# Branch A's first scores between the last q tiles, and denominators fetched by GpSimd and applied three tiles later

## The chip, the cores and the metric

The kernel runs on one core of a Trainium2 chip. The metric is device microseconds of one execution: the median of 3 runs was 1786.32 us (1786.25 to 1786.35). A core has five engines that each run their own queue in order: TensorE (PE; its weight loads, PEld, overlap its matmuls), VectorE (DVE), ScalarE (ACT), GpSimd (POOL) and SyncE (SP). In this kernel SP and POOL issue the transfers between the chip's memories. An instruction that waits holds up all that stands behind it in its queue.

## The reference, cut to what matters

One encoder layer over 1024 tokens of 1024 numbers. The change touches attention branch A:

```
h = RMSNorm(x);  z = h @ W_in                      # columns: A: q,k,v | B: q,k,v | gates
q = rope(rmsnorm(q)) * 128 ** -0.5                 # 8 heads of 128
k = rope(rmsnorm(k))                               # 2 heads of 128, each serves 4 q heads
pr = softmax(q @ k.T);  A = pr @ v                 # over all 1024 tokens
x += (sigmoid(gate_A) * (A @ W_oA) + sigmoid(gate_B) * (B @ W_oB)) @ W_o
```

Before it stand the projections and branch B, after it the output projections, the MLP and a gated embedding.

## The kernel before

All products are made in fp32r, three matmuls for one (`mm3`): each operand is split into a high part (a copy on ACT, line 236) and a low part (a subtraction on DVE, line 237), and all the matmuls of products stand at line 240.

`qkv_a` projects k and v of branch A (block 0) and then q in two blocks of four heads (blocks 1 and 2), each over 8 tiles of 128 tokens. A tile is 24 matmuls into one PSUM bank; ACT then squares it head by head (860) for the norm, and DVE applies the rotary tables (813, 818, 820). Two tiles later its `turn` runs: PE transposes it (834), ACT copies the result out of PSUM (839), SP stores it as `s_qd`. The banks of tiles are `ps_a`, those of turns `ps_t`. The last two turns are left over for the attention.

`attend_a` works through 16 units (8 heads times two halves of 512 queries), and a last pass without new scores. A unit has four score tiles: `scores(u, j)` is 6 matmuls, a maximum over 1024 scores on DVE (925), its product with the norm (927), an exponential on ACT (929) that fills a probability buffer and adds up a column of denominators. In pass u, step j, PE makes score tile j of unit u, then the transposes of two key chunks of unit u-1 (`weights`, 935, 8 matmuls; ACT and DVE split them, 236 and 237, tile `rp`), then the products with v of the two chunks before (`values`, 6 matmuls). The first transposes of unit u-1 need all four of its exponentials. `finish(u)` copies the unit's output out of PSUM (949), takes the reciprocal of its denominators (951), has SP store these as four columns to `s_rd` and load them back as one row on all partitions (`rb`), and then multiplies (956) and splits the result into `oA` (tile `ro`).

PE's order is the program's. The other engines' orders, and those of SP and POOL, are set by a scheduler from its own costs, so the text of the program does not show them. Tiles live in stacked regions on two sides of the on-chip memory; a region that is closed frees its place for the next one, which then waits for the readers of the old. In the kernel before, the score tiles' PSUM (banks 0 to 3) takes in the banks 2 and 3 of the turns.

## Time and profile before

| | |
|---|---|
| median of 3 runs | 1786.32 us |
| profiled execution, its own time | 1784.23 us |
| its span | 1782.5 us |
| PE busy in the span | 1734.3 us, 97% |
| DVE, ACT, POOL busy | 1255.6, 794.7, 391.1 us |
| tiles of q, block 2, until | 576.19 us |
| attention of branch A, unit to unit | 14.45 us |

Times inside the profile count from the span's start. A row of the timeline gives start and length in us, engine, line, operation, the tile written and the tiles read; in brackets stands how long the engine stood idle before it and what ended that. Matmuls are pipelined, so a group's length reaches a little into the next group's start; the chain that ended last cuts the groups without overlap. The clock (PEclk) is 1.00 at 2.4 GHz and 0.50 at 1.2 GHz.

### The profile page before, as it was taken

Reading aid. Unit: us, or ns where it says so; the run is one execution under the profiler, and the core shown is the slowest. Engines: PE = TensorE matmul, PEld = TensorE weight load, DVE = VectorE, ACT = ScalarE, POOL = GpSimd, SP = SyncE. Lnnn points to the kernel's source line nnn. Section 1 sums busy time; section 2 is a strip of 40 time slices with the busy share of each in tenths; the row PEclk is TensorE's granted clock in tenths of the full one; section 3 lists DMA queues with packets and bytes.
Section 4 is the critical chain, followed back from the end, with each engine's and each line's share of the span. In section 5 each row is a group of like instructions: output and inputs, shape, how many; then the busy total and the mean of one; then the engine's idle time right before and its main releaser. Section 6 shows DMA issues by size and latency. Waiting matters only on the chain.

```text
span 1782.5 us, 22922 instructions
## 1 busy us (share of the span) xinstructions
PE 1734.3 (97%) x8451; PEld 1434.9 (80%) x8451; DVE 1255.6 (70%) x2096; ACT 794.7 (45%) x1385; POOL 391.1 (22%) x242
## 2 busy tenths in 40 slices
PE   6999999999999899999999979999999999999997
PEld 5888888877888788888888868888888888888786
DVE  7546655476865888875446588667668999998664
ACT  6333334267333677775332346545547333330232
POOL 0242422010000000000001134322426677722000
PEclk9999999999999999999999989999999999999999
DMA  6243234476154322215433135656667222266111
GB/s 218 71 159 133 102 109 152 134 243 192 36 155 130 72 42 22 33 19 142 139 123 134 72 106 189 208 194 209 223 253 253 102 94 96 74 205 240 64 41 38
DMA packets 147552, 232.77 MB, mean 131 GB/s; under 512 B 27204, under 2 KB 94628, under 8 KB 147440
## 3 DMA queue, kind: packets, MB, share of 16 engines
q1 hardware_dynamic: 141152, 208.86, 36.7%
q0 software_dynamic: 6288, 22.44, 3.7%
q8 instruction: 67, 1.10, 0.3%
q14 instruction: 45, 0.37, 0.1%
HBM read 162.90 MB, written 71.51 MB: 132 GB/s over the span
## 4 chain that ended last, share of the span: by engine, by line
PE 65%; DVE 1%; issue 1%; ACT 0%; DVEq 0%; ACTq 0%
PE psum L240 61%; PE psum L935 3%; DVE rc L237 0%; PE psum L1370 0%; PE psum L1061 0%; ACT fp L929 0%; DVE base L925 0%; DVE hb L237 0%; ACT hb L236 0%; PE psum L1360 0%; DVE fx L1055 0%; DVE fsum L1306 0%; DVE fx L1077 0%; PE psum L834 0%; ACT rc L236 0%
## 5 line engine op out<-in xcount | busy, mean ns | idle before, releaser
L240 PE MATMUL psum<-rh,rh 128*128 128x512 f32 (+1 forms) x1428 | 336.2, 389 | 1.6 <-ACT rh L236 1.1
L240 PEld LDWEIGHTS psum<-rh,rh 128*128 128x128 f32 x1428 | 261.1, 190 | 59.5 <-issue 5.9
L240 PE MATMUL psum<-rc,rc 128*128 128x512 f32 x1320 | 304.2, 390 | 2.0 <-issue 1.6
L240 PEld LDWEIGHTS psum<-rc,rc 128*128 128x128 f32 x1320 | 246.7, 188 | 55.2 <-issue 4.2
L152 POOL TENSOR_TENSOR base<-base 128x512 f32<-128x512 f32 x17 | 25.9, 1525 | 776.8 <-DMA base<-in_w_ff 620.7
L240 PE MATMUL psum<-ht,rh 128*128 128x512 f32 x624 | 145.7, 389 | 0.0
L240 PE MATMUL psum<-hc,rc 128*128 128x512 f32 x576 | 137.9, 389 | 0.0
L240 PEld LDWEIGHTS psum<-ht,rh 128*128 128x128 f32 x624 | 117.1, 188 | 24.3
L236 ACT ACTIVATE rh<-base 128x512 fp32r<-128x512 f32 (+1 forms) x77 | 61.2, 808 | 147.9 <-PE psum L240 116.6
L240 PEld LDWEIGHTS psum<-hc,rc 128*128 128x128 f32 x576 | 108.1, 188 | 22.4
L237 DVE TENSOR_TENSOR rh<-base,rh 128x512 fp32r<-128x512 f32 (+1 forms) x77 | 77.4, 1014 | 62.6 <-PE psum L240 39.0
L240 PE MATMUL psum<-ro,rwt 128*128 128x512 f32 x480 | 109.0, 389 | 0.0
L240 PEld LDWEIGHTS psum<-ro,rwt 128*128 128x128 f32 x480 | 90.1, 188 | 18.7
L210 DVE TENSOR_TENSOR fw<-fw,psum 128x512 f32<-128x512 f32 x91 | 74.3, 817 | 43.6 <-PE psum L240 42.5
L240 PE MATMUL psum<-rp,kv 128*128 128x512 f32 x384 | 103.5, 405 | 0.0
L925 DVE TENSOR_REDUCE base<-psum 128x1 f32<-128x1024 f32 x64 | 78.3, 1224 | 35.6 <-PE psum L240 35.6
L240 PE MATMUL psum<-kv,rq 128*128 128x512 f32 x384 | 99.2, 395 | 2.5 <-ACT fp L929 1.6
L240 PE MATMUL psum<-hb,rc 128*128 128x512 f32 x384 | 94.6, 396 | 5.8 <-DVE hb L237 5.8
L1236 DVE TENSOR_TENSOR facc<-facc,psum 128x1024 f32<-128x1024 f32 x84 | 98.7, 1208 | 0.0
L237 DVE TENSOR_TENSOR rc<-fsum,rc 128x1024 fp32r<-128x1024 f32 x56 | 93.7, 1701 | 4.6 <-ACT rc L236 4.6
L236 ACT ACTIVATE rc<-fsum 128x1024 fp32r<-128x1024 f32 x56 | 57.4, 1055 | 85.3 <-issue 65.9
L240 PE MATMUL psum<-ha,rc 128*128 128x512 f32 x384 | 91.4, 394 | 0.0
(275 smaller groups left out, 3057.4 us busy)
## 6 DMA issues: line engine op xcount, KB each, us to landing
base<-in_w_ff SPq DMA_DIRECT2D x20, 1024.0 KB, 6.2
base<-in_w_in SPq DMA_DIRECT2D x13, 1024.0 KB, 5.1
base<-in_w_in SPq DMA_DIRECT2D x20, 512.0 KB, 4.7
s_u<-rfa SPq DMA_DIRECT2D x18, 512.0 KB, 2.9
fg<-s_gd SPq DMA_DIRECT2D x16, 512.0 KB, 5.9
s_wgs<-base SPq DMA_DIRECT2D x32, 256.0 KB, 2.0
s_gd<-fw SPq DMA_DIRECT2D x14, 512.0 KB, 3.1
rfa<-s_u SPq DMA_DIRECT2D x6, 1024.0 KB, 4.9
```

The costliest lines, as they stand in the source:

```text
L152: g.tensor_tensor(out=s1, in0=a21, in1=a22, op=ALU.add)
L210: self.nc.vector.tensor_tensor(out=self.c[out], in0=self.c[a], in1=self.p[i], op=op)
L236: self.nc.scalar.activation(hi, src, AF.Copy)
L237: (eng or self.nc.vector).tensor_tensor(out=lo, in0=src, in1=hi.bitcast(F32), op=ALU.subtract)
L240: self.nc.tensor.matmul(out, lhsT=lhsT, rhs=rhs, start=start, stop=stop)
L925: nc.vector.tensor_reduce(out=nm, in_=ps, axis=AX.X, op=ALU.max, negate=True)
L935: nc.tensor.transpose(pp[:, j * P:(j + 1) * P], probs[j][:, kc * P:(kc + 1) * P], self.ident)
L1236: v.tensor_tensor(out=o, in0=o, in1=ps, op=ALU.add)
```

## The change

Five things are edited. (1) `attend_a` becomes a generator that `qkv_a` advances in block 2 after the tiles 3 to 7: at tile 3 it takes its regions, and the four score tiles of unit 0 are made after the tiles 4, 5, 6 and 7. The loop then begins at unit 1. The load of head 0 moves from tile 3 to tile 2. (2) The q tiles get three banks (5 to 7) for four, turns one (4) for two; scores keep 0 to 3. Bank 4 is also the first of the three for transposes of probabilities. (3) Ten probability buffers for eight: two new ones, the two of `g_ring`, the four of `p_late` and the two rotary tables of q, whose region `fa` stays open. As the gain row of the MLP's norm lives in `g_ring`, its load comes after the attention. (4) The row `rb` is loaded by GpSimd's queue, into two buffers for three. (5) The multiplication and the split of a finished unit are put off: they are called at step 3 of the pass in which `finish` was called, and for the last unit in the first chunk of the output projection, whose orders on DVE and ACT are written out by hand.

```diff
--- before.py
+++ after.py
@@ -583,17 +583,17 @@
         self.p_late = [self.fp1.take(1024) for _ in range(4)]
         halves = [a[:, o:o + 512] for a in self.p_late for o in (0, 512)]
         t_ring, stage = Ring(halves[:6]), Ring(halves[6:])
-        fa = Region(tc, "fa", F32, "left")
-        mix = fa.take(512)
-        tabs = [v3(fa.take(1024), NT) for _ in range(2)] + tabs
+        self.fa = Region(tc, "fa", F32, "left")
+        mix = self.fa.take(512)
+        q_tabs = [self.fa.take(1024) for _ in range(2)]
+        tabs = [v3(a, NT) for a in q_tabs] + tabs
+        self.p_late += q_tabs
         beside = self.merge_b(qk[0], Ring([qk[1][:, :S]] + u_ring.slots))
+        attend = self.attend_a((fm, fq), rh)
         with tc.manual_schedule(engines={mybir.EngineType.PE}):
-            self.qkv_a(w_in, wt, hT, tabs, gtmp, t_ring, stage, lambda: self.weights_b(mix), beside)
-            fa.close()
-            fm.close()
-            fq.close()
-            rh.close()
-            self.attend_a()
+            self.qkv_a(w_in, wt, hT, tabs, gtmp, t_ring, stage, lambda: self.weights_b(mix), beside, attend)
+            for _ in attend:
+                pass
 
     def bias_rows(self, tmp, st, ps):
 
@@ -819,11 +819,11 @@
                                 in1=sin[:, a:a + 32].unsqueeze(1).to_broadcast([P, n, 32]), op=ALU.mult)
         v.tensor_tensor(out=t1[:, :w], in0=t1[:, :w], in1=t2[:, :w], op=ALU.add)
 
-    def qkv_a(self, w_in, wt, hT, tabs, gtmp, t_ring, stage, after_kv, beside):
+    def qkv_a(self, w_in, wt, hT, tabs, gtmp, t_ring, stage, after_kv, beside, attend):
 
         nc = self.nc
-        ps_a, ps_t = Ring(self.bank[4:]), Ring(self.bank[2:4])
-        self.ps_w = self.bank[1]
+        ps_a, ps_t = Ring(self.bank[5:]), Ring(self.bank[4:5])
+        self.ps_w = self.bank[3]
         q_tabs = self.rope_tables("q_norm_g", tabs[:2], gtmp, nc.vector)
         self.turns = []
 
@@ -875,8 +875,10 @@
                     after_kv()
                 if blk == 1 and t >= 4 or blk == 2 and t < 2:
                     next(beside)
-                if blk == 2 and t == 3:
+                if blk == 2 and t == 2:
                     self.load_q(0)
+                if blk == 2 and t > 2:
+                    next(attend)
             if blk:
                 x, r, tt = (a[:, 32 * blk - 32:32 * blk] for a in (self.qss, self.rq, self.qtmp))
                 nc.vector.tensor_scalar(x, x, 1.0 / DA, EPS, op0=ALU.mult, op1=ALU.add)
@@ -894,18 +896,16 @@
         self.split(q[0], q[1], raw)
 
 
-    def attend_a(self):
+    def attend_a(self, done, rh):
+
         tc, nc = self.tc, self.nc
-        self.ro = Region(tc, "ro", F32R, "right")
-        self.oA = [v3(self.ro.take(8192), HA) for _ in range(2)]
-        self.oB = [v3(self.ro.take(2048), 2) for _ in range(2)]
-        rp = Region(tc, "rp", F32R, "right")
-        pt_ring = rp.ring(6, 1024)
+        for region in done:
+            region.close()
         self.rq_pools.append(Region(tc, "rq1", F32R, "left"))
         self.qr.append([self.rq_pools[1].take(1024) for _ in range(2)])
         f0, fp = (Region(tc, n, F32, "left") for n in ("fp0", "fp"))
-        p_ring = Ring([f0.take(1024) for _ in range(4)] + self.p_late)
-        ou_ring, rb_ring = fp.ring(3, 512), fp.ring(3, 512)
+        p_ring = Ring([f0.take(1024) for _ in range(2)] + self.g_ring.slots + self.p_late)
+        ou_ring, rb_ring = fp.ring(3, 512), fp.ring(2, 512)
         den_ring = fp.ring(4, 8)
         s_ps, t_ps, o_ps = Ring(self.bank2[:2]), Ring(self.bank[4:7]), Ring(self.bank[7:])
 
@@ -952,14 +952,29 @@
             for j in range(4):
                 self.load(self.dr["rd"][u, j], rden[:, j:j + 1])
             rd = self.dr["rd"][u]
-            self.load(rb, bass.AP(tensor=rd.tensor, offset=rd.offset, ap=[[0, P], [1, 512]]))
-            nc.vector.tensor_tensor(out=ou, in0=ou, in1=rb, op=ALU.mult)
-            hs = slice(half * 512, half * 512 + 512)
-            self.split(self.oA[0][:, h, hs], self.oA[1][:, h, hs], ou)
+            nc.gpsimd.dma_start(rb, bass.AP(tensor=rd.tensor, offset=rd.offset, ap=[[0, P], [1, 512]]))
+
+            def scaled():
+                nc.vector.tensor_tensor(out=ou, in0=ou, in1=rb, op=ALU.mult)
+                hs = slice(half * 512, half * 512 + 512)
+                self.split(self.oA[0][:, h, hs], self.oA[1][:, h, hs], ou)
+            self.scaled.append(scaled)
 
         nu = 2 * HA
+        self.scaled = []
         dens = {u: None for u in range(nu)}
-        probs, late = None, []
+        probs, late = [], []
+        dens[0] = den_ring.next()
+        for j in range(4):
+            yield
+            probs.append(scores(0, j))
+        yield
+        rh.close()
+        self.ro = Region(tc, "ro", F32R, "right")
+        self.oA = [v3(self.ro.take(8192), HA) for _ in range(2)]
+        self.oB = [v3(self.ro.take(2048), 2) for _ in range(2)]
+        rp = Region(tc, "rp", F32R, "right")
+        pt_ring = rp.ring(6, 1024)
 
         def flush():
             while late:
@@ -968,7 +983,7 @@
                 if args[2] == NT - 1:
                     finish(args[0], args[3])
 
-        for u in range(nu + 1):
+        for u in range(1, nu + 1):
             nxt = []
             if u < nu:
                 dens[u] = den_ring.next()
@@ -977,17 +992,18 @@
                     nxt.append(scores(u, j))
                 if self.turns:
                     self.turns.pop(0)()
-                if u > 0:
-                    if j == 0:
-                        o = o_ps.next()
-                    new = [weights(u - 1, probs, kc, o) for kc in (2 * j, 2 * j + 1)]
-                    flush()
-                    late += new
+                if j == 3 and self.scaled:
+                    self.scaled.pop()()
+                if j == 0:
+                    o = o_ps.next()
+                new = [weights(u - 1, probs, kc, o) for kc in (2 * j, 2 * j + 1)]
+                flush()
+                late += new
             probs = nxt
             if u == 1:
                 self.merged_b()
         flush()
-        for region in (rp, fp, f0, self.rq_pools[1], self.fp1, self.rq_pools[0], self.kv):
+        for region in (rp, fp, f0, self.rq_pools[1], self.fa, self.fp1, self.rq_pools[0], self.kv):
             region.close()
 
     def merged_b(self):
@@ -1007,13 +1023,17 @@
         fg = Region(tc, "fg", F32, "right")
         g_ring = fg.ring(4, 1024)
         ps_r = Ring(self.bank2)
-        for c in range(KD):
+        E = mybir.EngineType
+
+        def chunk(c):
             wa = self.w_chunk(io["w_out_a"][0], c * P, wt)
             raw = v3(self.raw.next()[:, :256], 2)
             self.load(raw, io["w_out_b"][0][:, c * P:(c + 1) * P].rearrange("(k p) c -> p k c", p=P))
             wb = wt.next()
             wb = [v3(wb[:, 256 * i:256 * i + 256], 2) for i in range(2)]
             self.split(wb[0], wb[1], raw)
+            if c == 0:
+                self.scaled.pop()()
             ga, gb = g_ring.next(), g_ring.next()
             self.load(ga, self.dr["gd"][c])
             self.load(gb, self.dr["gd"][KD + c])
@@ -1028,6 +1048,11 @@
             nc.vector.tensor_tensor(out=ga, in0=ga, in1=ya, op=ALU.mult)
             nc.vector.tensor_tensor(out=gb, in0=gb, in1=yb, op=ALU.mult)
             nc.vector.tensor_tensor(out=m[:, c, :], in0=ga, in1=gb, op=ALU.add)
+
+        with tc.manual_schedule(engines={E.DVE, E.Activation}):
+            chunk(0)
+        for c in range(1, KD):
+            chunk(c)
         fg.close()
         self.ro.close()
 
```

Three places in the orders. On PE, the rows from the last q tile on: `rh` is the input and its weights, `kv` and `rq` are keys and queries (rows in which they are read are scores), 834 are turns, 935 transposes of probabilities. Before:

```order
L240 MATMUL psum_85<-rh_98,rh_90 128x512
L834 MATMUL psum_85<-base_58,fp_3159 128x128 x4
L240 MATMUL psum_85<-kv_3147,rq_3154 128x512 x2
L240 MATMUL psum_85<-kv_3148,rq_3154 128x512 x2
L240 MATMUL psum_85<-kv_3147,rq_3155 128x512 x2
L834 MATMUL psum_85<-base_58,fp_3160 128x128 x4
```

And now:

```order
L240 MATMUL psum_85<-rh_98,rh_90 128x512
L834 MATMUL psum_85<-base_58,fp_3159 128x128 x4
L240 MATMUL psum_85<-kv_3147,rq_3154 128x512 x2
L240 MATMUL psum_85<-kv_3148,rq_3154 128x512 x2
L240 MATMUL psum_85<-kv_3147,rq_3155 128x512 x2
L240 MATMUL psum_85<-kv_3147,rq_3154 128x512 x2
L240 MATMUL psum_85<-kv_3148,rq_3154 128x512 x2
L240 MATMUL psum_85<-kv_3147,rq_3155 128x512 x2
L834 MATMUL psum_85<-base_58,fp_3160 128x128 x4
L935 MATMUL psum_85<-base_58,fp_4176 128x128
```

Before, the three rows of scores behind the first turn are tile 0 of unit 0, and three more tiles of it and one of unit 1 follow with two turns ahead of the first 935. Now they are tile 3 of unit 0 and tile 0 of unit 1, and the first 935 comes after one more turn; the tiles 0 to 2 stand between the q tiles.

On DVE, the reciprocal of unit 0's denominators (`fp_4183`) and the rows around it; 254 to 259 and 884 or 886 are the norm of q's second block, 237 of `rq` the low part of a later head's queries. Now:

```order
L237 TENSOR_TENSOR rp_4412<-psum_85,rp_4412 128x512
L259 SCALAR_TENSOR_TENSOR base_72<-base_74,base_72 128x32
L951 RECIPROCAL fp_4183<-fp_4183 128x4
L886 TENSOR_SCALAR base_72<-base_72 128x32
L925 TENSOR_REDUCE base_67<-psum_85 128x1
L237 TENSOR_TENSOR rq_3155<-base_75,rq_3154 128x1024
L927 TENSOR_TENSOR base_67<-base_67,base_72 128x1
```

And the multiplication of unit 0 (958, was 956), which reads `rb` (`fp_4181`), in the second pass:

```order
L925 TENSOR_REDUCE base_69<-psum_85 128x1
L237 TENSOR_TENSOR rp_4411<-psum_85,rp_4411 128x512
L927 TENSOR_TENSOR base_69<-base_69,base_72 128x1
L237 TENSOR_TENSOR rp_4412<-psum_85,rp_4412 128x512
L958 TENSOR_TENSOR fp_4178<-fp_4178,fp_4181 128x512
L925 TENSOR_REDUCE base_70<-psum_85 128x1
L237 TENSOR_TENSOR rp_4407<-psum_85,rp_4407 128x512
L927 TENSOR_TENSOR base_70<-base_70,base_72 128x1
L237 TENSOR_TENSOR rp_4408<-psum_85,rp_4408 128x512
L237 TENSOR_TENSOR ro_4401<-fp_4178,ro_4400 128x512
L925 TENSOR_REDUCE base_63<-psum_85 128x1
```

Between unit 0's reciprocal and its multiplication stood 24 rows of DVE before; now there are 16, as the reciprocal comes after the low part of unit 0's sixth key chunk (`rp_4412`), where it stood ahead of unit 1's first maximum. For the units 1, 3, 5 and so on it is 24 rows now (21 before), for 2, 4 and so on 29 (26 before).

On SP, the stores and loads around unit 0's denominators, before and now in one piece of the difference:

```order
 L233 DMA s_qd<-fp_3162 128x4x128
 L233 DMA base_75<-s_qd 128x1024 x2
-L233 DMA s_rd<-fp_4377 128x1 x4
-L233 DMA fp_4374<-s_rd 128x512
-L233 DMA base_75<-s_qd 128x1024
-L233 DMA s_rd<-fp_4378 128x1 x4
-L233 DMA fp_4375<-s_rd 128x512
```

The stores stay on SP behind the loads of heads 4 and 5; the 16 loads of `rb` are gone from it and stand as 16 rows of line 955 on POOL, with nothing else of POOL's between its last memset of branch B and its first sum of the MLP.

## Rows read from the trace of the kernel before

**Rows 1.** Page, part 1: busy us (share of the span) x instructions.
```profile
PE 1734.3 (97%) x8451; PEld 1434.9 (80%) x8451; DVE 1255.6 (70%) x2096; ACT 794.7 (45%) x1385; POOL 391.1 (22%) x242
```

**Rows 2.** Timeline of PE from the last q tile to unit 0's first transposes.
```profile
576.19 0.60 PE L834 MATMUL psum<-base,fp 128*128 128x128 f32 x4
576.54 1.64 PE L240 MATMUL psum<-kv,rq 128*128 128x512 f32 x6
...
579.50 1.66 PE L240 MATMUL psum<-kv,rq 128*128 128x512 f32 x6 [0.88 <-ACT fp L839]
585.46 1.11 PE L834 MATMUL psum<-base,fp 128*128 128x128 f32 x4 [4.30 <-ACT fp L929]
586.23 4.09 PE L240 MATMUL psum<-kv,rq 128*128 128x512 f32 x12
591.92 1.68 PE L240 MATMUL psum<-kv,rq 128*128 128x512 f32 x6 [1.60 <-ACT fp L929]
593.44 1.03 PE L935 MATMUL psum<-base,fp 128*128 128x128 f32 x8
```

**Rows 3.** The chain that ended last, in the attention: start us, us, what.
```profile
606.73 0.87 PE psum L935 x8
607.60 2.74 PE psum L240 x12
...
621.18 0.87 PE psum L935 x8
```

**Rows 4.** Windows: us, busy of PE, PEld, DVE, ACT, POOL, PEclk, DMA share, GB/s.
```profile
585.40:588.00 2.60, 2.54 (x8) 2.24 (x9) 2.36 (x9) 0.61 (x2) 0.00 (x0) 0.50 0.48 187
590.40:593.40 3.00, 1.48 (x6) 1.19 (x7) 1.54 (x4) 2.59 (x4) 0.00 (x0) 1.00 0.84 287
1032.60:1035.00 2.40, 2.40 (x7) 1.91 (x6) 2.29 (x1) 2.37 (x4) 0.00 (x0) 0.50 0.23 87
```

**Rows 5.** Timeline of PE, a later wait.
```profile
1031.33 1.09 PE L1061 MATMUL psum<-base,fx 128*128 128x128 f32 x8 [3.50 <-DVE fx L1055]
```

**Rows 6.** Timeline of ACT and DVE after the last q tile.
```profile
577.78 0.23 ACT L860 ACTIVATION_READ_ACCUMULATOR fp<-psum 128x1 f32 x1
...
579.52 1.22 DVE L925 TENSOR_REDUCE base<-psum 128x1 f32<-128x1024 f32 x1
...
581.53 1.20 ACT L929 ACTIVATE fp<-psum,base,base 128x1024 f32<-128x1024 f32 x1 [0.19 <-DVE base L927]
```

**Rows 7.** Timeline, unit 15's last exponential and the transposes that wait for it.
```profile
805.50 1.23 DVE L925 TENSOR_REDUCE base<-psum 128x1 f32<-128x1024 f32 x1 [1.12 <-PE psum L240]
...
807.42 1.20 ACT L929 ACTIVATE fp<-psum,base,base 128x1024 f32<-128x1024 f32 x1 [0.34 <-DVE base L927]
...
808.77 0.77 PE L935 MATMUL psum<-base,fp 128*128 128x128 f32 x5 [0.73 <-ACT fp L929]
```

**Rows 8.** Timeline, two key chunks: transposes and the second chunk's low part.
```profile
595.70 1.03 PE L935 MATMUL psum<-base,fp 128*128 128x128 f32 x8
...
598.05 0.69 DVE L237 TENSOR_TENSOR rp<-psum,rp 128x512 fp32r<-128x512 f32 x1
```

**Rows 9.** Timeline of DVE and SP, denominators of unit 0: reciprocal, stores, load, multiplication.
```profile
593.26 0.18 DVE L951 RECIPROCAL fp<-fp 128x4 f32<-128x4 f32 x1 [1.42 <-ACT fp L929]
593.47 2.04 SPq L233 DMA_DIRECT2D s_rd<-fp  x4
...
602.99 0.32 SPq L233 DMA_DIRECT2D fp<-s_rd  x1
...
611.52 0.68 DVE L956 TENSOR_TENSOR fp<-fp,fp 128x512 f32<-128x512 f32 x1
```

**Rows 10.** DMA issues: out<-in, engine, count, KB each, median us to landing.
```profile
fp<-s_rd SPq DMA_DIRECT2D x16, 256.0 KB, 4.5
rg<-s_wgs POOLq DMA_DIRECT2D x10, 512.0 KB, 8.2
```

**Rows 11.** Tile s_vec, rows of 128x512 (256 KB) that GpSimd issued at 83 to 96 us.
```profile
L615 POOL DMA_DIRECT2D s_vec<-s_row x12: 523/523/570, 83.3 to 96.0; - x12
...
DMA to landing us min/median/max: 4.0/4.9/6.6
```

**Rows 12.** Timeline of DVE, the last unit's multiplication.
```profile
823.77 0.69 DVE L956 TENSOR_TENSOR fp<-fp,fp 128x512 f32<-128x512 f32 x1 [3.03 <-DMA fp<-s_rd]
```

**Rows 13.** Groups by line: busy us, mean ns, idle us before, releaser.
```profile
L237 DVE TENSOR_TENSOR rq<-base,rq 128x1024 fp32r<-128x1024 f32 x8 | 9.7, 1215 | 0.0
```

## Prediction

> **What bounds the kernel.** The page's busy times come first: PE works 97% of the span [rows 1], so an edit can only win where PE waits or runs at half clock, and lose where it makes PE wait. Next the chain that ended last: in the attention it is PE alone, 0.87 us of transposes and 2.74 us of products (two values or scores groups of 1.37 each) per step, 14.45 us from one unit's first transposes to the next (606.73 to 621.18) [rows 3]. A filled attention gives nothing back. So I read PE's timeline at the hand-over [rows 2]. The reader is to see that from the last q tile's end (576.19) to unit 0's first transposes (593.44) 17.25 us pass, in which PE does five score tiles and three turns: 5 x 1.37 + 3 x 0.44 = 8.2 us of work. Half of the stretch is lost: waits of 0.88, 4.30 and 1.60 us, all for ACT's reading of PSUM (score tiles and turns share banks), and matmuls at 1.2 GHz: the granted clock was 0.50 when PE resumed after the 4.30 [rows 4].
>
> **The hand-over, after.** I count from the end of the last q tile, at 576.19 before. After, three score tiles lie ahead of it between q tiles, where PE was full and stays full; their banks are their own, and DVE and ACT have room there, so they cost their own 3 x 1.37 = 4.1 us and zero is at 580.3. What would be lost if that cover were gone: the tiles' exponentials (3.5 us of DVE and ACT behind each rotary step) must end within a q tile's 5.9 us (24 matmuls at 2.74 / 12 and a turn), or the squares behind them slip. Then PE goes turn 0.44, score tile 3 to 1.81, tile 0 of unit 1 to 3.18, turn to 3.62, and its next work is unit 0's transposes, which need tile 3's exponential. That has a chain of its own: the last tile's squares end 1.82 us after the q tile (578.01), the rotary step lets the maximum start 1.5 us later, and from maximum to exponential it is 2.0 us, as in the kernel before [rows 6]; exponential to transposes is 1.35 [rows 7]. So the transposes start at 1.82 + 1.51 + 2.01 + 1.35 = 6.69: **PE still waits 3.1 us**, in one piece.
>
> From there: transposes 0.87, score tile 1.37, last turn 0.44, half the next transposes to 9.81. The other half needs bank 4, which the last turn has just filled; ACT's copy of it stands behind an exponential, and I put 0.5 us for the wait (0 to 1.35, one exponential). Then values, two steps of 3.61 and unit 2's first score tile: 20.71. Unit 1's transposes need its exponential 3, and there the new order puts the low part of a head's queries, 1.13 us (1.22 less overlap [rows 13]), between maximum and product, where a chunk's 0.66 stood. From maximum to transposes takes 3.27 us [rows 7], now 3.74: the score tile ends at 17.1, PE sees the exponential at 17.3 + 3.74 = 21.04 and waits 0.3. In the profile's time that is 601.34, where before it was 606.73 [rows 3]: **5.4 us won up to here**.
>
> **The row of denominators.** Before, unit 0's reciprocal ran at 593.26, its four stores were issued by 595.5, SP's load of the row could go at 602.99 (9.73 us after the reciprocal), and with 4.5 us to land [rows 10] it lay there at 607.5, 4.0 us before the multiplication wanted it (611.52) [rows 9]. So the wait was hidden by 24 rows of DVE. Now there are 16. The reciprocal comes after the low part of unit 0's sixth chunk: its transposes end at 14.4, and the low part is done 2.2 us after them (596.57 to 598.74 [rows 8]), so 16.5. The stores take the same way, so GpSimd can go at 26.3. What its load takes the trace doesn't show for this tile; the nearest row is GpSimd's own transfers of the same shape, 0.52 us of issue and 4.0 / 4.9 / 6.6 us from issue to landing [rows 11], against SP's 4.5. I take 4.9: the row is there at 31.2. DVE reaches the multiplication after unit 1's fourth chunk, 25.5 + 2.2 = 27.7. **It waits 3.5 us**, and behind it in DVE's queue stand the maximum of score tile 2, two chunks' low parts, unit 0's low part and the maximum of tile 3; ACT stops too, at unit 0's high part. From landing: 3.7 us for what stands ahead of tile 3's maximum (multiplication 0.68, maximum 1.22, three low parts of 0.68, a product, less 0.07 of overlap each), then 3.27 to the transposes of unit 2's pass: 38.2, where PE would be at 21.04 + 14.45 = 35.5. PE loses 2.7 us (1.8 to 4.4 for 4.0 to 6.6 us of landing; it hides only the first 0.8 of a late row). Later units have room: from reciprocal to multiplication it is one pass and one step for 1, 3, 5, 14.45 + 3.61 = 18.1 us (24 rows), more for the others, against 9.73 + 4.9 = 14.6. What remains: 5.4 - 2.7 = 2.7 us.
>
> The Trainium skill would make this cheaper: its page "DMA: Bandwidth & Descriptors" (Anatomy of one DMA, SWDGE path) fits a GpSimd transfer as 2.0 us plus bytes at 436 GB/s, an estimate of 2.6 us for 256 KB. By it the row would be 1.2 us late, PE would lose 0.4 us, and 5.0 would remain. No transfer of this shape in the trace landed under 4.0 [rows 11], so the sum keeps the row.
>
> **The clock.** After a wait of 3.50 us at 1031.33 the granted clock was 0.50 from 1032.6 to 1035.0, although PE worked again; after 4.30 us it was 0.50 at 585.4 to 588.0; after 1.60 us it stayed at 1.00 [rows 2, 4, 5]. The new wait of 3.1 us is nearer to 3.50, so I expect one fall. The rows show at least 2.4 to 2.6 us at half clock, which costs 1.2 to 1.3, and the fall's edges a little more: 1.4 (0 if it doesn't come; 2.8 if the second wait brings another). Before, the fall lay in the 17.25 us.
>
> **At no cost.** Three banks for four and one bank of turns for two: a q tile's last reader (rotary) is through about 3.4 us after it, the third next tile starts 11.8 us after it; a turn is copied before the next tile ends. The earlier load of head 0 and of head 1 (its place is now in freed memory) must be split by the end of tile 4, which leaves more than one q tile. If that cover fails, PE waits between q tiles. At the end, the last multiplication now waits for GpSimd (3.03 us before, for SP [rows 12]) with the first chunk's work behind it by hand; its reader is the last eighth of the first chunk's products, some 12 us after the attention's end, and the weights' splits are now ahead. The gain row is needed only 190 us later. More buffers give nothing, as PE never waited for one in the filled attention.
>
> **Sum.** 5.4 - 2.7 - 1.4 = 1.3 us won. The profiled execution took 1784.23 us (span 1782.5), 2.1 less than the median, so I take the difference to the median: 1786.3 - 1.3 = **1785.0**. With the bounds alone: 3.6 won (landing 4.0, no fall) to 1.8 lost (landing 6.6, two falls); 1782.7 to 1788.1.
>
> **Rivals.** (a) *The row is in time.* If GpSimd's transfer lands in 1.7 us or the stores land sooner without SP's load of other heads beside them, DVE's wait is under 0.8 and PE loses nothing: 5.4 - 1.4 = 4.0, 1782.3 (1780.9 without the fall). For it: POOL is idle there. Against it: the stores' 9.7 us are the larger part and don't change. (b) *The row is late for every second unit, and the kernel is slower.* GpSimd's 512 KB transfers took 8.2 us [rows 10]. From a landing of 6.2 us on unit 0 alone eats the 4.0 us; from 9.2 us on (18.1 - 9.7 + 0.8) the units 1, 3 ... 13 pay as well, seven times. At 10.5: DVE waits 9.1 at unit 0, PE 8.3; the others cost PE 1.3 each, 9.1; 4.0 - 17.4 = 13.4 slower, 1799.7. Against it: the shape's own row, 6.6 at most. (c) *The hand-over isn't filled*, because unit 0's transposes wait for the last tile's squares and rotary step whatever was moved: that is the 3.1 us above; if ACT's other work ahead of the exponential (two high parts of branch B's output and a turn's copy) adds 2 us more, with a second fall, nothing is left of the 1.3: 1787.
>
> Beside (b) stands a rule of the Trainium skill, on the page "SBUF — State Buffer" (SBUF: two separate sides): while DVE runs in a mode that takes the port it shares with GpSimd, GpSimd can't write the descriptors of its transfers. No row of this kernel shows it; by it the landing would be longer than the 4.9 of a stretch where DVE was less busy, towards (b).
>
> **How the numbers follow.** Forecast as worked out 0.48, (a) 0.27, (c) 0.14, (b) 0.11. A measurement of this kernel can tell about 0.2%, 3.6 us. Faster by more: most of (a) and the upper end of the forecast, 0.28. Slower by more: (b) where it goes beyond unit 0, and the end of (c), 0.10. The rest, 0.62, is no change. The range reaches into (a) and over (c): 1781.2 to 1788.6; the forecast's own is 1782.7 to 1788.1.
>
> **What would show it.** In the profile after: score groups between q tiles; one wait of about 3 us before unit 0's first transposes and no 4.30 ahead of a turn; PEclk 0.50 right after it; a multiplication (958) that waits 2 to 5 us for `s_rd` once, near 608, and two PE waits within 10 us of it; no other. Wrong if 958 never waits, if it waits in many units, or if q tiles show waits.

## The result, and the profile after

The changed kernel is slower. Its median is 1795.45 us (1792.26 to 1796.21, 4 runs); the kernel before took 1786.34 us on the same chip (4 runs). The ratio is 1.0055 with a 95% interval of 1.0042 to 1.0067, and 1785.0 was predicted. One execution each of e1 and e11 below, 1956 and 1948 us at a granted clock of 0.85, is left out of the figures. The profiled execution took 1795.76 us with a span of 1793.6, 11.1 more than before. The page's first part, busy time (share) x instructions, to be held against [rows 1]:

```profile
PE 1739.9 (97%) x8451; PEld 1437.7 (80%) x8451; DVE 1259.6 (70%) x2096; ACT 795.6 (44%) x1385; POOL 391.4 (22%) x258
```

PE has the same 8451 instructions, is busy 5.6 us longer and idle 5.5 us longer. So the loss shows in two ways, as waits and as the same work done more slowly. The waits of PE after, in total, times, longest:

```profile
PE psum L240 <- ACT rp L236: 5.2, 1, 5.2
PE psum L935 <- DVE rp L237: 4.5, 1, 4.5
...
PE psum L1086 <- DVE fx L1080: 3.5, 1, 3.5
```

The third stood there before (1061, [rows 5]). The other two are new. They took the place of the 4.30 and 1.60 us of [rows 2], and they lie elsewhere. The chain that ended last shows where the first of them comes from (start us, us, what):

```profile
600.95 1.02 PE psum L935 x8
...
607.05 7.14 DMA fp<-s_rd
...
614.22 0.70 DVE fp L958
...
616.84 1.12 PE psum L935 x4
617.96 3.65 PE psum L240 x12
621.61 0.87 PE psum L935 x8
```

Unit 1's first transposes come at 600.95 (606.73 in [rows 3]): the hand-over has won 5.8 us. Then the chain leaves PE for GpSimd's transfer of unit 0's row. Unit 2's transposes come at 621.61, where the kernel before had them at 621.18: **everything is given back within one unit**. The row on which this rests, of DVE's timeline (the bracket holds the idle time before it):

```profile
614.22 0.69 DVE L958 TENSOR_TENSOR fp<-fp,fp 128x512 f32<-128x512 f32 x1 [6.98 <-DMA fp<-s_rd]
```

The waits show no second unit like it.

The second place is the end of the attention, in the same view:

```profile
811.44 10.49 DMA base<-in_w_out_a
...
822.92 0.59 ACT rp L236
...
823.55 1.95 PE psum L240 x3
825.50 1.71 PE psum L935 x8
```

Here the chain runs through a load of weights of the *next* stage, then ACT's split of a key chunk, then PE. ACT's timeline says why (in brackets the idle time before a row):

```profile
814.07 0.59 ACT L236 ACTIVATE rp<-psum 128x512 fp32r<-128x512 f32 x1
814.55 0.42 ACT L236 ACTIVATE rwt<-base 128x256 fp32r<-128x256 f32 x1
821.96 1.06 ACT L236 ACTIVATE rwt<-base 128x1024 fp32r<-128x1024 f32 x1 [6.99 <-DMA base<-in_w_out_a]
822.92 0.58 ACT L236 ACTIVATE rp<-psum 128x512 fp32r<-128x512 f32 x1
```

Between two splits of probabilities (`rp`) stands a split of the third output chunk's weights (`rwt`), and ACT sits 6.99 us in front of it. The order of ACT there, before (the rows ahead are left out):

```
L236 ACTIVATE rp3_4352<-psum1_85 128x512
L236 ACTIVATE rp4_4353<-psum1_85 128x512
L236 ACTIVATE ro1_4343<-fp3_4373 128x512
L236 ACTIVATE rp5_4354<-psum1_85 128x512
L236 ACTIVATE rp6_4355<-psum1_85 128x512
L236 ACTIVATE rp1_4350<-psum1_85 128x512
L236 ACTIVATE rp2_4351<-psum1_85 128x512
L236 ACTIVATE rwt1_6326<-base14_75 128x1024
```

and after:

```
L236 ACTIVATE rp3_4409<-psum1_85 128x512
L236 ACTIVATE rwt6_6325<-base14_75 128x256
L236 ACTIVATE rwt7_6326<-base14_75 128x1024
L236 ACTIVATE rp4_4410<-psum1_85 128x512
L236 ACTIVATE ro1_4400<-fp3_4180 128x512
```

Before, all splits of weights stood behind the last chunk's; now those of the first two output chunks (`rwt6` is the last of them) stand here and further ahead, without a wait. The buffer `rwt7` lies in `fa`, which was another tenant's place before; now it is a probability buffer that unit 15 does not use, since 60 mod 10 is 0 and unit 15 takes the ring's first four. It is free early, and the scheduler puts its split early. The load that it needs is not early. SP, start and length of the issue:

```profile
811.44 0.38 SPq L233 DMA_DIRECT2D base<-in_w_out_a  x1
811.92 1.95 SPq L233 DMA_DIRECT2D s_rd<-fp  x4
813.97 0.38 SPq L233 DMA_DIRECT2D base<-in_w_out_b  x1
```

There are four staging buffers, all full with the first two chunks' weights since 752.96, and the first comes free when DVE has split the first chunk, at 811.41. The load goes out at 811.44 and lands 10.5 us later. (In the kernel before it went out later still, at 823.66, when PE was already at the output products.)

Last, the clock. Windows after: us, busy of PE, PEld, DVE, ACT, POOL, PEclk, DMA share, GB/s.

```profile
584.00:586.00 2.00, 0.79 (x6) 0.31 (x3) 2.00 (x5) 1.14 (x3) 0.00 (x0) 1.00 0.06 19
586.00:588.00 2.00, 1.04 (x7) 0.98 (x8) 2.00 (x4) 1.58 (x4) 0.00 (x0) 1.00 0.38 112
...
616.00:618.00 2.00, 1.16 (x5) 1.16 (x6) 1.96 (x6) 1.66 (x4) 0.00 (x0) 0.58 0.59 121
618.00:620.00 2.00, 2.00 (x6) 1.58 (x6) 2.00 (x5) 1.27 (x5) 0.00 (x0) 0.56 0.00 0
...
825.00:827.00 2.00, 2.00 (x11) 1.80 (x9) 2.00 (x3) 0.60 (x1) 0.00 (x0) 0.50 0.44 130
```

At the hand-over, where one fall was expected, it stayed at 1.00 (2.4 GHz). Behind each of the two new waits PE, back at work, ran at about half clock (1.2 GHz).

**The account by stretches.** The start of a program differs from one execution to the next: the last q tile ends 3.9 us apart over the thirteen profiles below. So kernels are compared stretch by stretch, from starts of groups in PE's timeline. Zero is the end of the last q tile (with old hand-overs, plus three score tiles, 4.11 us, which lay behind it). "Unit k" is the start of its first transposes. "Outputs" is the first unbroken run of output products. Where eight of them run inside the last pass, 8 x 0.228 us (137 took 31.27) are taken off the stretch before and added to the rest.

| kernel | zero at | zero to unit 1 | unit 1 to 2 | unit 2 to 15 | unit 15 to outputs | rest |
|---|---|---|---|---|---|---|
| before | 580.3 | 26.3 | 14.5 | 186.5 | 11.4 | 963.5 |
| after | 580.4 | 20.4 | 20.7 | 188.2 | 18.7 | 965.2 |
| e1 row_pool | 581.3 | 21.7 | 14.6 | 188.5 | 18.0 | 967.9 |
| e2 end_turned | 580.9 | 21.7 | 21.4 | 188.2 | 11.4 | 967.4 |
| e3 both | 578.0 | 20.4 | 14.7 | 188.2 | 11.4 | 965.3 |
| e4 row_sp | 578.3 | 20.3 | 15.8 | 189.1 | 10.9 | 966.4 |
| e5 scores_only | 578.7 | 20.3 | 20.2 | 186.5 | 11.4 | 966.4 |
| e6 row_gpsimd_only | 577.4 | 26.3 | 14.5 | 186.5 | 11.4 | 968.0 |
| e7 row_sp_turned | 578.9 | 20.4 | 16.3 | 189.1 | 11.4 | 967.7 |
| e8 stores_held | 580.6 | 22.0 | 16.3 | 189.3 | 18.8 | 966.2 |
| e9 load_early | 577.8 | 20.4 | 22.0 | 186.6 | 10.9 | 968.5 |
| e10 pool_load_early | 580.2 | 21.7 | 14.6 | 188.7 | 10.9 | 965.2 |
| e11 pool_ring8 | 578.7 | 20.3 | 14.6 | 186.6 | 11.4 | 965.0 |

After against before: 5.9 won at the hand-over, 6.2 lost at unit 0's row, 1.7 in the filled attention, 7.3 at its end, which makes 9.3 lost; the medians differ by 9.1. The rest (965.2 against 963.5) varies as much among kernels that are alike there, 963.5 for the kernel before and 968.0 for e6: PE is idle 12.4 us in the one and 16.2 in the other, by waits of 1 us and less that come and go from profile to profile.

### The profile page after: what moved, and what is told of

Its sections match the earlier page's. It is cut to its first block, busy times and chain, and to the rows that moved or that the text cites. A ratio compares the mean times of both kernels' runs of the same rounds, so it can differ in the third digit from the quotient of the medians.

```text
span 1793.6 us, 22949 instructions
## 1 busy us (share of the span) xinstructions
PE 1739.9 (97%) x8451; PEld 1437.7 (80%) x8451; DVE 1259.6 (70%) x2096; ACT 795.6 (44%) x1385; POOL 391.4 (22%) x258
## 4 chain that ended last, share of the span: by engine, by line
PE 60%; DVE 11%; issue 2%; DMA 1%; ACT 1%; DVEq 0%; ACTq 0%
PE psum L240 56%; DVE rc L237 6%; DVE facc L1261 4%; PE psum L935 3%; DMA base<-in_w_out_a 1%; PE psum L834 0%; PE psum L1086 0%; PE psum L1395 0%; DMA fp<-s_rd 0%; DVE base L925 0%; DVE hb L237 0%; ACT rp L236 0%; ACT fm L731 0%; ACT hb L236 0%; DVE rp L237 0%
## 5 line engine op out<-in xcount | busy, mean ns | idle before, releaser
L240 PEld LDWEIGHTS psum<-ro,rwt 128*128 128x128 f32 x480 | 90.0, 188 | 18.8 <-ACT rwt L236 0.3
L955 POOL DMA_DIRECT2D fp<-s_rd x16 | 8.7, 542 | 436.5 <-DVE base L927 239.2
```

Source lines behind the costliest of these rows:

```text
L240: self.nc.tensor.matmul(out, lhsT=lhsT, rhs=rhs, start=start, stop=stop)
L955: nc.gpsimd.dma_start(rb, bass.AP(tensor=rd.tensor, offset=rd.offset, ap=[[0, P], [1, 512]]))
```

## The experiments

The theory: two instructions that wait in the queues of DVE and ACT, one for unit 0's row and one for the third chunk's weights, make the loss. The rivals: the loss is spread over longer steps; GpSimd's queue is slow as such; the early scores themselves cost it. A ratio is to runs of the kernel before beside it on the same chip. The chip was one for e1 to e4, another for e5 to e8 and a third for e9 to e11 (medians of the kernel before: 1786.75, 1786.33 and 1785.90 us).

**e1, unit 0's row out of DVE's queue.**

```diff
+                if u == 0:
+                    nc.gpsimd.tensor_tensor(out=ou, in0=ou, in1=rb, op=ALU.mult)
+                    nc.gpsimd.tensor_copy(hi, ou)
+                    nc.gpsimd.tensor_tensor(out=lo, in0=ou, in1=hi.bitcast(F32), op=ALU.subtract)
+                    return
...
```

(and GpSimd's order is that of the text, with unit 0 called a pass later, so that unit 1's row is issued ahead of it).

> The changed kernel, but GpSimd does unit 0's multiplication and split, after it has issued unit 1's row, so that no DVE or ACT instruction waits for unit 0's row of denominators; all else as in the changed kernel. Theory (two queue stalls make the loss): the 7.0 us wait of the multiplication near 607 and PE's wait of 4.46 us at 616.84 go, with the half clock behind it; unit 2's first transposes come at 615.2 to 615.7 where they came at 621.45; about 6 us back, 1789.5 (1788.5 to 1790.5). PE's wait of 5.2 us at the attention's end stays. Rival (the row is late for the other units too, since the stores of unit 1 took 11 us): DVE waits at unit 1's multiplication instead, and 2 us or less come back, 1793.5 or more. Rival (the loss is spread over the longer steps of 3.65 us): under 1 us back.

Measured: 1789.87 us (1779.3 to 1793.7), ratio to before 1.0003 (0.9988 to 1.0019). Unit 1 to 2 takes 14.6 us, no multiplication waits, and the wait at the end is still there (4.0 us). Unit 2's transposes come at 617.6 and not by 615.7, since zero lies 0.9 later and a clock fall adds 1.3 at the hand-over, but their distance to unit 1's is the expected one. The row itself was no sooner (KB, us to landing):

```profile
fp<-s_rd POOLq DMA_DIRECT2D x1, 256.0 KB, 7.6
```

So the stall at unit 0 is the waiting in DVE's queue. The wide range of this kernel's times (two runs at 1779 to 1780) would fit an end that stalls in some executions only, as e4 will suggest; the profile is of one that stalled.

**e2, the order at the end.**

```diff
+            if u in (3, 6, 9):
+                p_ring.next(), p_ring.next()
```

> The changed kernel with ten probability buffers still, but the ring skips two of them at units 3, 6 and 9, so that unit 15 uses the last four (two of fp1, two of fa) instead of the first four. The weights' splits of the output projection then stand behind the last chunks' splits on ACT and DVE, as in the kernel before. Theory: PE's wait of 5.2 us near 823 and the half clock behind it go; about 7 us back, 1788.4 (1787.4 to 1789.6); the multiplication's 7.0 us wait near 607 stays. Rival (the load of the third chunk of w_out_a is late whatever the order): the wait moves to the first output products, and 2 us or less come back, 1793.5 or more.

Measured: 1790.60 us, ratio 1.0022 (1.0013 to 1.0031). ACT has its order of before, and all splits of weights follow the last `rp`:

```profile
820.72 1.09 ACT L236 ACTIVATE rp<-psum 128x512 fp32r<-128x512 f32 x2 [1.11 <-PE psum L935]
821.69 2.62 ACT L236 ACTIVATE rwt<-base 128x1024 fp32r<-128x1024 f32 x4
```

From unit 15 to the outputs it takes 11.4 us again: the expected 7.3 are back. The median gives only 4.9 back and lies 1.0 above the range expected, with 1.3 of a clock fall at the hand-over and 2.2 more in the rest of this profile against it.

**e3, both edits.**

> Both edits together. Theory: both stalls gone, 1795.4 - 6 - 7 = 1782.4 with steps of 3.65 us, 1780.5 if the steps are 3.61 again; faster than the kernel before by 4 to 6 us. Rival (spread loss, or the hand-over's 5.9 us are given back elsewhere): 1786 or more.

Measured: 1780.63 us, ratio 0.9966 (0.9954 to 0.9978). The diffs are those of e1 and e2. From 590 us to the end of the attention PE now waits once:

```profile
PE psum L935 <- ACT fa L929: 0.7, 1, 0.7
```

That wait stood there before as well (0.73 in [rows 7]). The hand-over's gain is real and is kept when the two stalls are out. The rival of a spread loss falls as the main cause: the steps are still 3.65 us here, for which 1782.4 was written, so 1780.63 is not the doing of shorter steps.

**e4, the row by SP's queue again.**

```diff
-            nc.gpsimd.dma_start(rb, bass.AP(tensor=rd.tensor, offset=rd.offset, ap=[[0, P], [1, 512]]))
+            self.load(rb, bass.AP(tensor=rd.tensor, offset=rd.offset, ap=[[0, P], [1, 512]]))
```

> The changed kernel with the row of denominators loaded by SP's queue again, as in the kernel before. Theory (the 7.0 us are mostly the stores' way, which SP had in both kernels, and 2 to 3 us GpSimd's transfer): the row lands 3 us sooner, DVE waits about 3.5 to 4 us, PE loses 2.5 to 3 in place of 6: 1792 (1791 to 1793.5). Rival (GpSimd's queue makes the whole wait): no wait near 607, 1789.5. Rival (the queue doesn't matter): 1795.4.

Measured: 1781.86 us, ratio 0.9976 (0.9966 to 0.9985): 10 us better than expected. The first half came as written. The row landed 4.5 us after its issue, and DVE waited

```profile
608.65 0.69 DVE L958 TENSOR_TENSOR fp<-fp,fp 128x512 f32<-128x512 f32 x1 [3.52 <-DMA fp<-s_rd]
```

PE lost 2.0 us by it, counted against e3 from unit 1 to 15: 1.1 in this unit and 0.9 in the next, where one more wait of 0.65 stands for unit 2's last exponential, whose maximum had been held up behind the multiplication. The second half was not foreseen: the stall at the end is gone, with ACT's and DVE's orders as in the changed kernel. The load of the third chunk was issued 0.43 us ahead of the last unit's column stores, as there (0.48), and landed in 3.7 us in place of 10.5:

```profile
base<-in_w_out_a SPq DMA_DIRECT2D x1, 512.0 KB, 3.7
```

```profile
809.14 1.06 ACT L236 ACTIVATE rwt<-base 128x1024 fp32r<-128x1024 f32 x1 [0.22 <-DMA base<-in_w_out_a]
```

So the misplaced split costs only what its load is late, and that is not the same every time.

**e5, the early scores alone.** Of the changed kernel only parts 1 and 2: SP loads the row (e4's line), the hand-written order of the first output chunk is gone, and

```diff
-        p_ring = Ring([f0.take(1024) for _ in range(2)] + self.g_ring.slots + self.p_late)
+        p_ring = Ring([f0.take(1024) for _ in range(2)] + self.g_ring.slots + self.p_late[:4])
...
-            self.scaled.append(scaled)
+            scaled()
```

> The first scores between the q tiles and the bank split alone (parts 1 and 2), with the row loaded by SP, the multiplication called at once and eight probability buffers, unit 15 in fp1 as in the kernel before. Theory: the hand-over wins its 6 us, nothing waits at the attention's end, but unit 0's multiplication now stands 13 rows of DVE behind its reciprocal (16 in the changed kernel, 24 before), so with a row at 9.7 + 4.5 = 14.2 us after it DVE waits about 5.5 us and PE loses 4.5: unit 2's first transposes 1 to 2 us ahead of the kernel before, 1785.2 (1783.5 to 1787.5, the upper end if steps take 3.65 us). Rival (the early scores alone win it all): no wait, 1780.5. Rival (the early scores are what makes the kernel slower): 1790 or more.

Measured: 1785.82 us, ratio 1.0002 (0.9993 to 1.0011), as expected. The multiplication, one step earlier than in the changed kernel, waits 5.1 us:

```profile
609.36 0.69 DVE L958 TENSOR_TENSOR fp<-fp,fp 128x512 f32<-128x512 f32 x1 [5.11 <-DMA fp<-s_rd]
```

Zero to unit 1 wins 6.0, unit 1 to 2 loses 5.7: nothing is left. The early scores bring their gain and, by the reciprocal's new place, take it back.

**e6, the row by GpSimd alone**, in the kernel before (e4's line, the other way round).

> The kernel before with nothing changed but the row's load, which goes to GpSimd's queue (part 4). Theory: unit 0's row takes 7 to 8 us to land, as it flies beside unit 1's column stores, but has 24 rows of DVE to do so, so at most 1 us is waited for it; the others land in 3.3 to 4.1 us; 1786.5, no difference (1785.5 to 1788). Rival (a load by GpSimd costs time whatever the order): waits at several multiplications, 1789 or more.

Measured: 1788.30 us (1781.4 to 1792.0), ratio 1.0007 (0.9993 to 1.002), no difference, and no wait in the attention that the kernel before lacks. One number was expected wrongly: unit 0's row landed in 3.7 us, not 7 to 8. In this order unit 1's column stores go out at 606.50, after that row has landed (600.38 + 3.7), so it has no company. A load by GpSimd is not slow as such.

**e7, SP's queue and the turned ring**, the diffs of e4 and e2.

> The changed kernel with the row loaded by SP and the ring turned so that unit 15 uses the last four buffers: both stalls out, without GpSimd. Theory: as the run with both edits, 1780 to 1781.5, and 1 us or less under the run with SP's load alone, whose profile showed no stall at the end. Rival (the turned ring costs something of its own): 1783 or more.

Measured: 1785.63 us (1781.7 to 1788.9), ratio 0.9999 (0.9989 to 1.0008): 4 us or more above what was expected. By its profile the ring costs nothing at the end (11.4 us) and unit 0's row costs 2.5 from unit 1 to 15 (a wait of 3.99). What is more than in e3 beyond that lies in stretches that the edit doesn't touch: zero 0.9 later, 2.4 in the rest. Why its median is 3.8 above e4's, which ran on another chip, is not settled.

**e8, unit 1's stores held back** until unit 0's row has landed, by two small copies on GpSimd ahead of them (executed once).

```diff
+            rows.append(rb)
+            if u == 1:
+                nc.gpsimd.tensor_copy(hold[:, 0:4], rows[0][:, 0:4])
+                nc.gpsimd.tensor_copy(hold[:, 0:4], rden)
+                rden = hold[:, 0:4]
```

> The changed kernel, but unit 1's four column stores are held back until unit 0's row has landed (two small copies on GpSimd between them); a look at one transfer. Theory (unit 0's row takes 7 to 8 us because unit 1's column stores fly beside it): it lands in 3.3 to 4.5 us like the 15 others, and unit 0's multiplication waits 3.5 to 4.5 us in place of 7.0; unit 1's own row comes late instead and DVE waits for that. Rival (it is slow as the first transfer of GpSimd's queue after 228 us of nothing): still 7 to 8 us.

Measured: 1794.96 us, a single execution, from which only the transfer is read. The landing of unit 0's row and the second unit's in the changed kernel, then of unit 0's row here (KB each, us to landing):

```profile
fp<-s_rd POOLq DMA_DIRECT2D x1, 256.0 KB, 7.1
fp<-s_rd POOLq DMA_DIRECT2D x1, 256.0 KB, 3.5
```

```profile
fp<-s_rd POOLq DMA_DIRECT2D x1, 256.0 KB, 4.0
```

```profile
613.01 0.69 DVE L964 TENSOR_TENSOR fp<-fp,fp 128x512 f32<-128x512 f32 x1 [3.97 <-DMA fp<-s_rd]
```

Without unit 1's stores beside it the row lands in 4.0 us and the wait falls from 7.0 to 4.0 (row of e8 above). In the changed kernel the 15 other rows landed in 3.3 to 4.1, none with stores beside it. The rival (first use of the queue) falls, here and by e6, where the first row landed in 3.7.

**e9, the third chunk's load early**, with the orders of ACT and DVE unchanged: the small loads of `w_out_b` for the chunks 0 and 1 share a staging buffer.

```diff
-            raw = v3(self.raw.next()[:, :256], 2)
+            if c != 1:
+                self.raw_b = self.raw.next()
+            raw = v3(self.raw_b[:, 256:512] if c == 1 else self.raw_b[:, :256], 2)
```

> The changed kernel with its orders on ACT and DVE, but the two small loads of w_out_b for the first two output chunks share one staging buffer, so that the third chunk's w_out_a has a buffer free and is loaded long before the attention's end. Theory (the stall at the end is the wait for that load, which in the changed kernel can only be issued at 811): PE's wait of 5.2 us and the half clock behind it go though the splits still stand ahead of the last chunks' splits; about 7 us back, 1788.4 (1787 to 1790.5); unit 0's stall stays. Rival (the splits' own 1.1 us each ahead of the last chunks make it): PE still waits 2 us or more there, 1792 or more.

Measured: 1787.83 us, ratio 1.0013 (1.0004 to 1.0022). The load goes out at 750.55, and ACT passes the misplaced splits without a wait:

```profile
811.61 1.37 ACT L236 ACTIVATE rwt<-base 128x256 fp32r<-128x256 f32 x2
812.86 0.60 ACT L236 ACTIVATE rp<-psum 128x512 fp32r<-128x512 f32 x1
```

Unit 15 to outputs: 10.9 us. The order as such costs nothing; the wait for a late load in it cost 7.3 to 7.8.

**e10, e1 and e9 together.**

> The same early load, and GpSimd does unit 0's multiplication and split: both stalls out with the order at the end as in the changed kernel. Theory: as with the ring turned, 1780.6 (1779 to 1783). Rival (the order at the end costs by itself): 1784 or more.

Measured: 1779.67 us (1778.9 to 1783.1), ratio 0.9966 (0.9954 to 0.9977): as fast as e3, by another way of taking out the second stall. These two and e4, which had the row's wait but not the stall at the end, beat the kernel before clear of the runs' spread, by 0.2 to 0.3%.

**e11, e1 with eight probability buffers**, the ring of e5.

> GpSimd does unit 0's multiplication and split, and the ring has eight probability buffers, without the two in fa, so that unit 15 lies in fp1 as in the kernel before (part 3 undone). Theory (more buffers give nothing, and cost the stall at the end): 1780.6, no wait at the end. If the steps of 3.65 us come from the ring of ten, they are 3.61 here and it is 1778.7; if they are set by chance at a pause of PE, either.

Measured: 1784.25 us, ratio 0.9986 (0.9975 to 0.9997). By stretches it is the best of all (14.6, 186.6, 11.4, rest 965.0, profiled execution 1778.25), but that execution is the fastest of its runs. Their median lies 3.7 above the 1780.6 expected and the slowest at 1787, and the profile doesn't say why.

## Why the prediction was wrong

**The step that failed** stands in "At no cost": at the end, "the weights' splits are now ahead", at a price of nothing. The order after showed the splits ahead of the last chunks' splits. That was read as work moved out of the way, and it was not asked when their loads could land. The third chunk's load needs a staging buffer that is free only at 811.4, and ACT and DVE stop in front of its split with PE's next operands behind it. It cost 7.3 us (5.2 of waiting, the rest half clock and what follows). e2 (order) and e9 (load) each take it out; either alone is enough. This is the larger part of the 10.5 us by which the forecast missed. By stretches it is about 7.3 here, 2.1 at unit 0's row (6.2 for the 2.7 and the 1.4 of clock that were written), 1.7 in longer steps, less 0.5 won more at the hand-over. Without it the kernel is still no faster: e9, where it is out, took 1.0013 of the kernel before (1.0004 to 1.0022).

**The row of denominators: the mechanism was right, a term was too small.** Written: reciprocal at 596.8, DVE at the multiplication at 608.0, wait 3.5. Measured: 596.40, 607.24, wait 6.98. The stores' way was 10.65 us where 9.73 had been seen, and the landing 7.1 where 4.9 was taken (0.9 and 2.2 of the 3.5 that were missing; DVE's earlier arrival, less the earlier reciprocal, is the rest). The landing was taken from rows of the same shape, but from device memory to device memory, and with no column stores beside them [rows 11]. The change itself brings the company: unit 1's reciprocal now runs 7 us after unit 0's (16 before), so its stores are ready before unit 0's row is; on SP they stood behind the row's load, and with the load on another queue they go ahead of it. For PE, 2.7 us of 3.5 was somewhat too much, since e4 lost 2.0 at a wait of 3.5 and e7 2.5 at 4.0 without a clock fall, and 6.2 at 7.0 came with one.

**The hand-over** was right: 5.8 us against 5.4, with some luck in the sum. The waits written (3.1 for the last exponential, 0.5 for bank 4, 0.3 at unit 1) came as 1.43, as 0.74 and 0.25 (ACT's copies of turns out of bank 4), and as under 0.2; the exponential's was short since the transposes of the three early tiles' keys went ahead of the fourth's. That is 1.3 us less of waiting, of which only 0.5 shows in the time to unit 1: the work between took 0.8 longer than written. **The clock** fell behind the two new waits, where no fall had been priced, and not here; in four of the eleven kernels with the new hand-over (e1, e2, e8, e10) it did fall here, at 21.7 to 22.0 in place of 20.4, which is the 1.4 written.

**Not foreseen** were the longer steps of the filled attention, 1.7 us (their cause is open, see below). What the text put at nothing beside the end held: no q tile waited, no head's load, the gain row or the last multiplication cost anything that a wait shows.

**The rivals.** (a), the row in time: false, the row was later than written and not sooner. (Its condition of 1.7 us should read 2.2 by the prediction's own numbers, 27.7 + 0.8 - 26.3.) (b): its mechanism, a late landing, came, but for unit 0 alone, since 3.3 to 4.1 us leave the later units their room. (c): false. Of the two pages named, the Trainium skill's "DMA: Bandwidth & Descriptors" (SWDGE path) gave an estimate of 2.6 us for the transfer; no run landed one under 3.27. The rule of the Trainium skill's "SBUF — State Buffer" (SBUF: two separate sides) holds GpSimd's transfers up while DVE runs in a mode that takes the shared port. No row shows in which mode DVE ran; with DVE 80% busy (153 of the 190 us from 620 on) the transfers landed in 3.3 to 4.1, sooner than SP's 3.9 to 5.3 in the kernel before, so no run here shows it.

## What to carry to other kernels

An instruction that a scheduler moves ahead is free only if its data are there: for each that now stands ahead of work on the path, find the load that it waits for, what frees that load's buffer, and when. A transfer moved to a queue of its own no longer holds back what stood behind it, so its time must be taken from rows with that company ahead of them. And a gain at a hand-over is worth what the next unit lets through: here one late row took all of it.

## What the runs showed of the hardware

**A landing told late.** The column stores (128 x 1 numbers each) took 6.7 to 10.2 us from issue to landing in the changed kernel. Unit 0's row, issued behind the four of unit 1, landed after 7.1 us (7.3 to 8.1 in e1, e2, e3, e9, e10 and e11), the 15 others after 3.3 to 4.1. Its bytes were not slower. Windows of the changed kernel ahead of its landing at 614.20, the two columns at the right DMA share and GB/s:

```profile
609.00:610.00 1.00, 1.00 (x7) 0.83 (x6) 0.00 (x0) 0.00 (x0) 0.00 (x0) 1.00 0.51 139
610.00:611.00 1.00, 1.00 (x6) 0.84 (x5) 0.00 (x0) 0.00 (x0) 0.00 (x0) 1.00 0.09 37
611.00:612.00 1.00, 1.00 (x8) 0.79 (x7) 0.00 (x0) 0.00 (x0) 0.00 (x0) 1.00 0.00 0
612.00:613.00 1.00, 0.38 (x4) 0.14 (x2) 0.00 (x0) 0.00 (x0) 0.00 (x0) 1.00 0.00 0
613.00:614.00 1.00, 0.00 (x0) 0.00 (x0) 0.00 (x0) 0.00 (x0) 0.00 (x0) 1.00 0.00 0
```

From 611 on, 4 us after the row's issue, nothing moves, and DVE stands idle three us more. In all seven profiles the landing comes 0.15 to 0.18 us after that of the last of unit 1's stores (614.03 here). So it was the notice of the row's landing that came late, behind the stores', and not the row itself; why is open. The next row does the same where it went out beside unit 2's stores: 7.8, 7.1 and 6.9 us in e1, e10 and e11. Issued 0.4 to 0.5 us ahead of the stores it did not wait for them: unit 0's row by SP in e4, e5 and e7, 4.5 to 5.2 us, and the second row in e3, 3.4.

The 512 KB load issued just ahead of such stores landed in 10.5 us after, 9.3 in e1, 10.9 in e8, 3.7 in e4. In the first of these the bytes had moved as fast as in the last. Windows of the changed kernel:

```profile
812.00:813.00 1.00, 1.00 (x7) 0.82 (x6) 0.48 (x2) 1.00 (x3) 0.00 (x0) 1.00 0.33 98
813.00:814.00 1.00, 1.00 (x8) 0.87 (x7) 1.00 (x2) 0.98 (x3) 0.00 (x0) 1.00 1.09 329
814.00:815.00 1.00, 1.00 (x7) 0.78 (x7) 1.00 (x3) 0.97 (x3) 0.00 (x0) 1.00 0.65 100
...
821.00:822.00 1.00, 0.00 (x0) 0.00 (x0) 0.00 (x0) 0.04 (x1) 0.00 (x0) 0.56 0.53 18
```

98 + 329 + 100 GB/s over three us are 527 KB, in 1025 packets of 512 B, of which the load is 1024, and yet its landing came at 821.93. The some 20 GB/s of the seven us between are the next loads'; the stores hold 0.5 KB each. What decides whether a load's landing comes with its bytes, as in e4, or with the stores' is open.

**Two lengths of a step.** A score matmul has one of two median durations, with nothing else changed (min/median/max ns, first and last start):

```profile
L240 PE MATMUL psum<-kv,rq x290: 389/394/398, 624.6 to 799.9; 128*128 128x512 f32 x145
L240 PE MATMUL psum<-kv,rq x18: 389/389/393, 603.2 to 611.5; 128*128 128x512 f32 x18
```

Both rows are of the changed kernel, the first behind and the second ahead of its wait at 616.84. The steps are 3.65 us with the one and 3.61 with the other, and where they changed, PE had paused. In the kernel before, e5, e6, e9 and e11 they were 3.61 from unit 2 on or soon after it, in after, e2, e3, e4 and e7 3.65; in e1 and e10 they went from 3.61 to 3.65 at a wait of 0.2 to 0.3 us near 632, in e8 from 3.65 to 3.61 at one of 1.2 near 636. e9 has the ring of ten and the waits of unit 0, so neither sets it. Its cost is up to 2 us; its cause is open.

**The clock after like waits.** The same waits of 0.74 and 1.43 us at the hand-over were followed by a granted clock of 1.00 in the changed kernel and of 0.69 in the same window of e1 (first the changed kernel's, then e1's). What sets the one or the other is open.

```profile
588.00:590.00 2.00, 1.98 (x13) 1.48 (x11) 2.00 (x8) 2.00 (x4) 0.00 (x0) 1.00 0.36 68
588.00:590.00 2.00, 2.00 (x10) 1.67 (x10) 2.00 (x6) 1.81 (x3) 0.00 (x0) 0.69 0.15 16
```
